# Decoder block on one core: the projection of q, k and v with the weights stationary, its row of factors by transposes, and the rotated rows moved by DMA

## The chip, the cores and the metric

The kernel runs on 1 core of one Trainium2 chip. The metric is the device time of an execution in microseconds (us), the median of the runs. TensorE (PE) multiplies, VectorE (DVE), ScalarE (ACT) and GpSimd (POOL) work on what lies beside it, and the queues of SP, ACT and POOL issue DMAs.

## What is computed

One layer on 1024 rows of width 1024: RMSNorm, one wide projection, a pooling mixer beside a sliding-window attention with sinks, merged by gates, and an MLP with squared ReLU. What the change touches is the projection to q, k and v, the partial rotation, and how they reach the attention:

```python
h = _rmsnorm(x, g_mix_pre[l])
proj = jnp.einsum('bsd,de->bse', h, w_in[l]) + b_in[l]
u_pool, q, k, v, gates = jnp.split(proj, IN_SPLITS, axis=-1)
q = _partial_rotary(q.reshape(B, S, N_Q_HEADS, HEAD_DIM), cos, sin)   # first 16 of 64 dims
k = _partial_rotary(k.reshape(B, S, N_KV_HEADS, HEAD_DIM), cos, sin)
v = v.reshape(B, S, N_KV_HEADS, HEAD_DIM)
y_attn = _sliding_window_sink_attention(q, k, v, attn_sinks[l])       # 8 q heads, 2 kv heads
```

## The kernel before

Every float32 operand is split into a high and a low part (`split`: a cast on ACT, a difference on DVE), and each product is made in three passes (`PASSES`). x comes transposed (`xt`, eight tiles k of 128 features by 1024 rows), is scaled by the norm's gain and split (`scaled`, L201 to L204). The norm's factor of each row, `r1`, is not known yet: the sums of squares come from a second read of x by rows (`square_row`, L211), and the factor is put in where the products leave PSUM.

**The projection.** `mm_q` (L178) and `mm_kv` (L188) take a tile n of 128 rows of x as the stationary operand and stream the weights: 512 columns for q, 256 for k and v. The loop over k (L216 on) does this for n = 0 to 3 as the tiles arrive. The products lie with the rows on the partitions. `pre_q` and `pre_kv` (L311, L314) multiply by the row's factor, a scalar of each partition, and add the bias; `rotate` turns the first 16 dims of each head, on DVE for n = 0 and on POOL for the others; `post_qkv` (L339) transposes q (four, L344) and k (one, L345) with PE, so that the features come to lie on the partitions, splits them, and prepares v on POOL. `make_rb` writes the eight factors of each partition to DRAM and reads them back as one row `rb` on all partitions, for the gates.

**The order.** Behind the loop the order on PE, DVE and ACT is that of the code (`manual_schedule`). The attention of tile n is `score_all(n)` (L388), `softmax_max`, `softmax_exp`, `softmax_scale` (L420), `attend_t` (transposes of the probabilities, L431), `attend_own`, `attend_v` (L456). Between these, `fill(t)` takes work for PE from the stream `others()`: the projection of n = 4 to 7, then halves of the gates' products (`half`, L583 through `gt.mm`), until about t us are spent. In step n of the loop stand `attend_t(n)`, the exponentials and the scale of n + 1, `attend_v(n)`, the scores of n + 2, and `post_qkv(n + 3)`.

Of the kernel before, what the change touches and what calls it, by code (L numbers as in the profile page):

```python
# [8 lines left out]
F32 = mybir.dt.float32  # L9
# [27 lines left out]
C_COS = C_MASK + 2 * P  # L37
C_SIN = C_COS + NT * 8
C_CNT = C_SIN + NT * 8
# [7 lines left out]
V_N = V_ONE + 1  # L47
# [3 lines left out]
def block_kernel(ctx: ExitStack, tc, xt, x, consts, vecs, sinks, b_qkv, g_post, g_mlp, g_mlp_post,  # L51
# [95 lines left out]
    cst = cp.tile([P, C_N], F32, name="cst")  # L147
# [32 lines left out]
    def mm_q(n, k, bq):  # L180
        for j, (xh, h) in enumerate(PASSES):
            pe.matmul(bq, xs_[k][n // 4][:, xh, n % 4 * P:(n % 4 + 1) * P], wq[k][:, h, :],  # L182
                      start=k == 0 and j == 0, stop=k == NK - 1 and j == 2)

    def bkv_of(n):
        return bkv[n // 2 * 2][:, n % 2, :] if n < 4 else bkv[n][:, 0, :]

    def mm_kv(n, k, joint=False):  # L188

        for j, (xh, h) in enumerate(PASSES):  # L190
            pe.matmul(bkv_of(n), xs_[k][n // 4][:, xh, n % 4 * P:(n % 4 + 1) * P],  # L191
                      wkv[k // 2][:, h, k % 2, :], start=k == 0 and j == 0 and not (joint and n % 2),
                      stop=k == NK - 1 and j == 2 and not (joint and n % 2 == 0))

    bq01, bq23 = bank("sc", [2, 512]), bank("sc", [2, 512])
    bq = {0: bq01[:, 0, :], 1: bq01[:, 1, :], 2: bq23[:, 0, :], 3: bq23[:, 1, :]}
    bz = bank("mm")
    bkv = {0: bank("mm", [2, 256]), 2: bank("mm", [2, 256])}
    for j in range(9):
        pe.matmul(bz, zeros[:, :P], zeros, start=j == 0, stop=j == 8)  # L200
    def scaled(t, xs, gk, th, a, b):  # L201
        src = xs[:, th * 512 + a:th * 512 + b]
        act.activation(t[:, 0, a:b], src, AF.Identity, scale=gk)
        dve.scalar_tensor_tensor(t[:, 1, a:b], src, gk, f32(t[:, 0, a:b]), ALU.mult, ALU.subtract)  # L204


    later = []

    ssq = small()

    def square_row(n):  # L211
        t = at(*(("qkv", 3) if n % 2 == 0 else ("s4", 4)), [S])
        nc.sync.dma_start(t, x[n])
        act.activation(t, t, AF.Square, accum_out=ssq[:, n:n + 1])

    for k in range(NK):  # L216
        xs = at("s4", 4, [S])
        ws = stage([768]) if k else ws_first
        if k < 2:
            if k == 0:  # L220
                nc.sync.dma_start(vec, vecs)
            for a, b in ((0, 256), (256, 512)) if k == 0 else ((0, 512),):
                nc.sync.dma_start(xs[:, a:b], xt[k][:, a:b])
            if k:
                nc.sync.dma_start(ws, w_qkv[k])
            else:
                nc.sync.dma_start(ws[:, 512:], w_qkv[k][:, 512:])
            later.append((k, xs))
        else:
            nc.sync.dma_start(xs, xt[k])  # L230
            nc.sync.dma_start(ws, w_qkv[k])
            if k == 2:
                for i, t in later:
                    nc.sync.dma_start(t[:, 512:], xt[i][:, 512:])
        halves_ = [xp.tile([P, 2, 512], F32R, tag="x", name=nm("x")) for _ in range(2)]
        gk = vec[:, V_G + k:V_G + k + 1]
        q = wslot([2, 512]) if k < 6 else ga_.tile([P, 2, 512], F32R, tag="ga", name=nm("wq"))
        if k % 2 == 0:
            wkv.append(ga_.tile([P, 2, 2, 256], F32R, tag="ga", name=nm("wkv")))
        kv = wkv[-1]  # L240
        first = k == 0
        if first:
            split(q[:, 0, :], q[:, 1, :], ws[:, :512], first=dve)
        for a, b in ((0, 256), (256, 512)) if first else ((0, 512),):
            scaled(halves_[0], xs, gk, 0, a, b)
        if not first:
            split(q[:, 0, :], q[:, 1, :], ws[:, :512])
        split(kv[:, 0, k % 2, :], kv[:, 1, k % 2, :], ws[:, 512:])
        if k >= 2:
            scaled(halves_[1], xs, gk, 1, 0, 512)  # L250
        xs_.append(halves_)
        wq.append(q)
        for n in range(4):
            mm_q(n, k, bq[n])
        for n in range(4):
            mm_kv(n, k, joint=True)
        if k == 2:
            for i, t in later:
                scaled(xs_[i][1], t, vec[:, V_G + i:V_G + i + 1], 1, 0, 512)
        if k >= 5:  # L260
            square_row(k - 5)
    for n in range(3, NT):
        square_row(n)
    nc.sync.dma_start(cst, consts)
    nc.sync.dma_start(snk, sinks.unsqueeze(0).broadcast_to([P, NH]))
    bq_b = bcast(b_qkv, 768)
    dve.tensor_scalar(nsnk, snk, -1.0, None, ALU.mult)
# [35 lines left out]
    tfs = {}  # L303

    def tf_of(n):
        if n not in tfs:
            tfs[n] = flat(yy.tile([P, 2, 512], F32, tag="y", name=nm("tf"))) if n in (2, 3, 7) else at("qkv", 3, [1024])
        return tfs[n]

    def pre_q(n):  # L310
        dve.scalar_tensor_tensor(tf_of(n)[:, :512], bq[n], r1[:, n:n + 1], bq_b[:, :512], ALU.mult, ALU.add)  # L311

    def pre_kv(n):
        dve.scalar_tensor_tensor(tf_of(n)[:, 512:768], bkv_of(n), r1[:, n:n + 1], bq_b[:, 512:768], ALU.mult, ALU.add)  # L314

    def rotate(n):
        tf = tf_of(n)
        t = tf[:, :768].rearrange("p (h d) -> p h d", d=HD)
        c = cst[:, C_COS + 8 * n:C_COS + 8 * n + 8].unsqueeze(1).unsqueeze(1).broadcast_to([P, 10, 2, 8])
        s = cst[:, C_SIN + 8 * n:C_SIN + 8 * n + 8].unsqueeze(1).unsqueeze(1).broadcast_to([P, 10, 2, 8])  # L320
        rot = t[:, :10, :ROT].rearrange("p h (a b) -> p h a b", a=2)
        a = tf[:, 768:928].rearrange("p (h a b) -> p h a b", a=2, b=8)
        b = sp.tile([P, 10, 2, 8], F32, tag="rb", name=nm("rb"), bufs=1)
        eng = pool if n else dve
        eng.tensor_tensor(a, rot, c, ALU.mult)
        eng.tensor_tensor(b, rot, s, ALU.mult)
        eng.tensor_tensor(rot[:, :, 0, :], a[:, :, 0, :], b[:, :, 1, :], ALU.subtract)
        eng.tensor_tensor(rot[:, :, 1, :], a[:, :, 1, :], b[:, :, 0, :], ALU.add)

    vfs = {}  # L330
# [8 lines left out]
    def post_qkv(n):  # L339
        tf = tfs.pop(n)  # L340
        t = tf[:, :768].rearrange("p (h d) -> p h d", d=HD)
        bt, bk = bank("mm"), bank("mm")
        for m in range(4):
            pe.transpose(bt[:, m * P:(m + 1) * P], tf[:, m * P:(m + 1) * P], ident)  # L344
        pe.transpose(bk[:, :P], tf[:, 512:640], ident)  # L345
        qt = at("qt", 2, [2, 512], F32R)
        split(qt[:, 0, :], qt[:, 1, :], bt)
        ks = slice(n * P, (n + 1) * P)
        split(khi[:, ks], klo[:, ks], bk[:, :P])
        qts[n] = qt  # L350

# [380 lines left out]
    def others():  # L732
        for n in range(4, NT):
            bq[n] = bank("mm")
            for k in range(NK):
# [4 lines left out]
                if k == NK - 1:  # L740
                    pre_q(n)
# [1692 lines left out]
```

## Time and profile before

| | us |
|---|---|
| runs of the kernel before (3) | 1086.58, 1087.01, 2804.63; median 1087.01 |
| the profiled execution's own time | 1086.91 |
| its span, first to last instruction | 1085.1 |
| mean granted TensorE clock | 0.998 of full speed |
| busy: PE, DVE, ACT, POOL | 1076.7, 891.9, 635.5, 102.9 |
| DMA, mean over the span | 223 GB/s |

The span is what the profiler saw of the program's instructions; the time also has what lies around it. A timeline row gives an instruction's start and length, and how many of a kind follow one another; as matmuls and many others overlap their successors, the distance from start to start prices a stream. Groups give busy time and the mean length of one. One of the three runs stands far from the other two; the median does not use it.

### The profile page before, as it was taken

The page shows a single profiled execution, that of the slowest core. Times are in us where ns is not written, and L with a number is a line of the kernel's source. Part 1 is how long each engine was busy: PE and PEld are TensorE (multiplying, and loading weights), DVE is VectorE, ACT ScalarE, POOL GpSimd, SP SyncE. Part 2 cuts the span into 40 slices and gives each one's busy share as a digit, 9 for nine tenths or more (in the row PEclk, how much of TensorE's full clock was granted, in tenths as well). Part 3 has the DMA queues.
Part 4 walks back from the last instruction along what each step waited for, and adds up shares of the span by engine and source line. Part 5 has one row for each costly group of instructions (what it writes and reads, how often), then busy time and mean ns, then how long its engine had stood idle before and what let it go on. Part 6 is the DMA issues. An engine that isn't in the chain of part 4 may idle for free.

```text
span 1085.1 us, 14912 instructions
## 1 busy us (share of the span) xinstructions
PE 1076.7 (99%) x5355; PEld 907.9 (84%) x5355; DVE 891.9 (82%) x1294; ACT 635.5 (59%) x1058; POOL 102.9 (9%) x174
## 2 busy tenths in 40 slices
PE   9999999999999999999999999999999999999997
PEld 8888888888888888888888888888888899899886
DVE  6688888989887887879979867776757899898997
ACT  7567886456654247587666555555544474275553
POOL 0354410100100012100000000001000000000000
PEclk9999999999999999999999999999999999999999
DMA  9656899679865776822576654655898687459842
GB/s 339 200 170 176 214 250 349 191 233 312 260 216 178 220 200 137 291 84 92 191 253 242 251 207 161 227 184 212 294 393 274 217 274 255 151 175 331 300 140 78
DMA packets 106618, 242.06 MB, mean 223 GB/s; under 512 B 11056, under 2 KB 28592, under 8 KB 106544
## 3 DMA queue, kind: packets, MB, share of 16 engines
q1 hardware_dynamic: 86528, 191.69, 51.6%
q0 software_dynamic: 14112, 29.37, 11.5%
q10 hardware_dynamic: 5904, 20.06, 4.7%
q8 instruction: 42, 0.69, 0.2%
q14 instruction: 32, 0.26, 0.1%
HBM read 166.63 MB, written 73.40 MB: 221 GB/s over the span
## 4 chain that ended last, share of the span: by engine, by line
PE 94%; DVE 2%; ACT 2%; DMA 1%; issue 1%; SPq 0%; DVEq 0%; ACTq 0%
PE mm L583 26%; PE at L583 19%; PE at L2129 12%; PE mm L2129 5%; PE mm L1523 5%; PE at L2103 4%; PE mm L2103 4%; PE mm L494 3%; PE sc L182 2%; PE at L1523 2%; PE at L1251 2%; PE mm L191 2%; PE mm L182 2%; PE mm L1251 2%; PE mm L496 1%; PE sc L456 1%
## 5 line engine op out<-in xcount | busy, mean ns | idle before, releaser
L2129 PE MATMUL at<-ar,wh 128*128 128x512 f32 x564 | 134.6, 389 | 0.0
L2129 PEld LDWEIGHTS at<-ar,wh 128*128 128x128 f32 x564 | 105.8, 188 | 22.2 <-DVE ar L104 0.3
L101 ACT CAST wh<-raw 128x1024 fp32r<-128x1024 f32 (+1 forms) x54 | 53.4, 988 | 79.9 <-PE at L2129 51.3
L104 DVE TENSOR_TENSOR wh<-st,wh 128x512 fp32r<-128x512 f32 (+1 forms) x106 | 76.4, 730 | 25.0 <-ACT wh L101 21.2
L583 PE MATMUL mm<-T,wx 128*128 128x512 f32 x375 | 90.9, 390 | 0.0
L104 DVE TENSOR_TENSOR wh<-raw,wh 128x1024 fp32r<-128x1024 f32 (+1 forms) x54 | 61.6, 1142 | 29.4 <-ACT wh L101 29.1
L583 PEld LDWEIGHTS mm<-T,wx 128*128 128x128 f32 x375 | 70.2, 188 | 15.1 <-DVE wx L104 0.6
L101 ACT CAST wh<-st 128x512 fp32r<-128x512 f32 (+2 forms) x105 | 67.6, 653 | 19.4 <-DVE st L539 5.8
L583 PE MATMUL mm<-gr,wh 128*128 128x512 f32 x321 | 77.4, 391 | 0.0
L583 PEld LDWEIGHTS mm<-gr,wh 128*128 128x128 f32 x321 | 59.9, 188 | 12.2
L2129 PE MATMUL mm<-ar,wh 128*128 128x512 f32 x276 | 69.6, 389 | 0.0
L583 PE MATMUL mm<-T,wh 128*128 128x512 f32 x267 | 66.1, 389 | 0.0
L101 ACT CAST ar<-B 128x1024 fp32r<-128x1024 f32 (+2 forms) x59 | 43.0, 757 | 30.7 <-PE mm L2129 14.8
L2129 PEld LDWEIGHTS mm<-ar,wh 128*128 128x128 f32 x276 | 51.8, 188 | 10.7
L583 PE MATMUL at<-gr,wh 128*128 128x512 f32 x243 | 59.0, 389 | 0.0
L583 PEld LDWEIGHTS mm<-T,wh 128*128 128x128 f32 x267 | 50.1, 188 | 10.5
L583 PE MATMUL mm<-x,wh 128*128 128x512 f32 x240 | 58.9, 394 | 0.0
L583 PEld LDWEIGHTS at<-gr,wh 128*128 128x128 f32 x243 | 45.6, 188 | 9.5
L583 PEld LDWEIGHTS mm<-x,wh 128*128 128x128 f32 x240 | 44.2, 188 | 9.6 <-ACT f L692 0.2
L583 PE MATMUL at<-T,wx 128*128 128x512 f32 x213 | 52.2, 389 | 0.0
L104 DVE TENSOR_TENSOR ar<-B,ar 128x1024 fp32r<-128x1024 f32 (+2 forms) x59 | 49.1, 855 | 1.1 <-ACT ar L101 1.1
L2103 PE MATMUL at<-ar,wh 128*128 128x256 f32 x336 | 47.5, 283 | 0.0
(556 smaller groups left out, 2461.2 us busy)
## 6 DMA issues: line engine op xcount, KB each, us to landing
raw<-f_dram SPq DMA_DIRECT2D x40, 512.0 KB, 4.2
B<-in_w_dn_dram SPq DMA_DIRECT2D x32, 512.0 KB, 6.6
st<-in_w_up_dram SPq DMA_DIRECT2D x27, 512.0 KB, 5.0
f_dram<-g SPq DMA_DIRECT2D x21, 512.0 KB, 2.9
wh<-f_dram SPq DMA_DIRECT2D x20, 512.0 KB, 5.8
g<-spill_dram SPq DMA_DIRECT2D x17, 512.0 KB, 6.0
st<-in_w_g_dram SPq DMA_DIRECT2D x16, 512.0 KB, 5.0
f_dram<-g ACTq DMA_DIRECT2D x16, 512.0 KB, 3.8
```

Of the source, the lines that this page charges most:

```text
L101: act.copy(hi, src)
L104: return eng.tensor_tensor(lo, src, f32(hi), ALU.subtract)
L182: pe.matmul(bq, xs_[k][n // 4][:, xh, n % 4 * P:(n % 4 + 1) * P], wq[k][:, h, :], start=k == 0 and j == 0, stop=k == NK - 1 and j == 2)
L191: pe.matmul(bkv_of(n), xs_[k][n // 4][:, xh, n % 4 * P:(n % 4 + 1) * P], wkv[k // 2][:, h, k % 2, :], start=k == 0 and j == 0 and not (joi ...
L456: pe.matmul(yb[:, kv], v[:, c:c + P], p[ph][:, 4 * kv:4 * kv + 4].rearrange("p i q -> p (i q)"), start=j < 2, stop=j >= len(mms) - 2)
L494: pe.matmul(bs[th], whi[:, k, :], rhs(k, hl, th), start=k == 0 and hl == 0, stop=False)
L496: pe.matmul(bs[th], wlo[:, k, :], rhs(k, 0, th), start=False, stop=k == nk - 1)
L583: pe.matmul(b, w[wh][:, kt, :], x_, start=not after and kt == 0 and j == 0, stop=kt == 3 and j == 2, skip_group_check=after)
L1251: pe.matmul(b, w[wh][:, kt, :], xo[xh][:, kt, :], start=not after and kt == 0 and j == 0, stop=kt == 1 and j == 2, skip_group_check=after)
L1523: pe.matmul(bs[t], Am[a][k][ah][:, t * P:(t + 1) * P], Wm[w][k][wh], start=not after and k == 0 and j == 0, stop=k == 3 and j == 2, skip_g ...
L2103: pe.matmul(part[q][:, t, :], o[fs][fh][:, fk, t * P:(t + 1) * P], o[ws][wh][:, wk, :], start=q not in onto and (s_, t, j) == (0, 0, 0), s ...
L2129: pe.matmul(bs[t], fo[fh][:, k2, t * P:(t + 1) * P], wo_[wh][:, k2, :], start=not after and s2 == 0 and k2 == 0 and j == 0, stop=(s2, k2) ...
```

## The change

The columns of the projection are put into six groups f of 128 features, and the weights are the stationary operand (`mm_in`): a product is 128 features by 512 rows, so q and k lie with features on the partitions from the start and are not transposed. Groups 0 to 3 hold the parts of two q heads that are not rotated, 48 and 48, with 32 features of v between them; groups 4 and 5 hold the first and second halves of the rotated dims of all heads (80 features each) and 48 of the rest of k. The first 512 rows (th = 0) are projected while the tiles arrive, the others (th = 1) in `others()`.

Because a row's factor now varies along the free dimension, the row `rb` is needed ahead of the first product that leaves PSUM. `factors(th)` makes the factors of half th and spreads them, and `make_rb(th)` turns them into a row on all partitions by four transposes. `close_in` multiplies by it (DVE) and adds the bias, one per partition (ACT). `turn` and `turn_end` rotate groups 4 and 5 as a whole, on DVE for th = 0 and on POOL for th = 1. The rotated rows then move by DMA (`rows_in`, `keys_rest`) into the places between the others that v's rows held, after v's have been moved (`values_out`) to a tile `tv`; for th = 0 v is read from a tile of its own (`unbiased`), which holds the products ahead of the bias. `split_q(n)` splits q of 128 rows, `split_k` k of 512, and `post_v` transposes v, once per tile. Tables of the rotation come from a new input; the tile of `cst` keeps its old size without them, and the tiles behind it their addresses.

```diff
+    def mm_in(f, th, k, a=0, b=512):
+        for j, (wh, xh) in enumerate(PASSES):
+            pe.matmul(b_in[f, th][:, a:b], w_in_of(f, k, wh), xs_[k][th][:, xh, a:b],
+                      start=k == 0 and j == 0 and a == 0, stop=k == NK - 1 and j == 2)
...
+    def factors(th):
+        n = slice(4 * th, 4 * th + 4)
+        rsqrt(r1[:, n], ssq[:, n], 4)
+        t = rows_of[th] = at("s4", 4, [2, 512])[:, 0, :]
+        dve.tensor_copy(t.rearrange("p (n k) -> p n k", k=P), r1[:, n].unsqueeze(2).broadcast_to([P, 4, P]))
+
+    def make_rb(th):
+        b, t = bank("mm"), rows_of.pop(th)
+        for n in range(4):
+            pe.transpose(b[:, n * P:(n + 1) * P], t[:, n * P:(n + 1) * P], ident)
+        act.copy(rb[:, th * 512:(th + 1) * 512], b)
...
+        for f in (4, 5, 0, 1):
+            for k in (6, 7):
+                mm_in(f, 0, k)
+        nc.sync.dma_start(cst, consts)
         for n in range(4):
+            square_row(n, at("qkv", 3, [S]) if n < 3 else at("s4", 4, [S]))
+        load_table(0)
+        factors(0)
...
+    def close_in(f, th):
+        raw_in(f, th)
+        t = o = raw_of(f, th)
+        if f < 4 and not th:
+            if f % 2 == 0:
+                unbiased[f // 2] = wide_s8()
+            t = unbiased[f // 2][:, f % 2]
+        dve.tensor_tensor(t, b_in.pop((f, th)), rb[:, th * 512:(th + 1) * 512], ALU.mult)
+        act.activation(o, t, AF.Identity, bias=vec[:, V_BQ + f:V_BQ + f + 1])
...
+    def turn(th, eng):
+        t, tab = raw_r[th][:NR], tables.pop(th)
+        turned[th] = [at("s4", 4, [2, 512])[:NR] for _ in range(2)]
+        for i, o in enumerate(turned[th]):
+            eng.tensor_tensor(o, t, tab[:NR, i, :].unsqueeze(1).broadcast_to([NR, 2, 512]), ALU.mult)
+
+    def turn_end(th, eng):
+        t, (a, b) = raw_r[th][:NR], turned.pop(th)
+        eng.tensor_tensor(t[:, 0], a[:, 0], b[:, 1], ALU.subtract)
+        eng.tensor_tensor(t[:, 1], a[:, 1], b[:, 0], ALU.add)
+
+    MOVES = ((0, 0, 16, 56), (1, 0, 8, 48), (1, 8, 16, 72))
+
+    def rows_in(q, th, dst, m):
+        for i, a, b, to in MOVES:
+            q.dma_start(dst[to:to + b - a], raw_r[th][16 * m + a:16 * m + b, i, :])
...
+    def split_q(n):
+        qt = qts[n] = at("qt", 2, [2, 512], F32R)
+        for i, src in enumerate(raw_q[n // 4]):
+            hi, lo = (qt[:, h, i * 256:(i + 1) * 256].rearrange("p (m k) -> p m k", k=P) for h in range(2))
+            split(hi, lo, src[:, :, n % 4 * P:(n % 4 + 1) * P])
...
     def others():
-        for n in range(4, NT):
-            bq[n] = bank("mm")
+        for f in (4, 5, 0, 1, 2, 3):
+            b_in[f, 1] = bank("mm")
             for k in range(NK):
-                mm_q(n, k, bq[n])
+                mm_in(f, 1, k)
...
+                    close_in(f, 1)
+                    if f == 5:
+                        keys_rest(nc.sync, 1)
+                        turn(1, pool)
+                        turn_end(1, pool)
+                        rows_in(nc.sync, 1, raw_k[1], 4)
+                    elif f < 4:
+                        values_out(nc.sync, 1, f)
+                    if f in (1, 2, 3):
+                        rows_in(nc.sync, 1, raw_of(f - 1, 1), f - 1)
+                    if f == 1:
+                        split_k(1)
...
-        rsqrt(r1, ssq[:, :NT], NT)
-        make_rb()
+        make_rb(0)
+        for f in (2, 3):
+            for k in (6, 7):
+                mm_in(f, 0, k)
+        for n in range(4, NT):
+            act.activation(squares_late[n], squares_late[n], AF.Square, accum_out=ssq[:, n:n + 1])
+        close_in(4, 0)
+        close_in(5, 0)
+        turn(0, dve)
+        keys_rest(nc.sync, 0)
+        turn_end(0, dve)
+        rows_in(nc.sync, 0, raw_k[0], 4)
+        for m in range(4):
+            close_in(m, 0)
+            rows_in((nc.sync, nc.scalar, nc.scalar, nc.gpsimd)[m], 0, raw_of(m, 0), m)
+        for m in range(4):
+            values_out(nc.gpsimd, 0, m)
+        load_table(1)
+        factors(1)
+        fill(4.0)
+        make_rb(1)
         act.activation(warm, r1[:, :1], AF.Exp)
...
+        split_k(0)
+        fill(6.5)
+        split_q(0)
+        fill(1.6)
         score_all(0)
...
                 hurry[0] = False
+                if n + 2 < NT:
+                    split_q(n + 2)
...
-            if n + 3 < NT:
-                post_qkv(n + 3)
+            if n + 2 < NT:
+                post_v(n + 2)
```

TensorE between the end of the first half's projection and the first transposes behind it, before. `mm_502` and `mm_529` are tile 4 of q and of k and v; `mm_551` and `mm_552` are the transposes of tile 0:

```order
L191 MATMUL mm_102<-wkv_365,x_405 128x256 x6
L182 MATMUL mm_502<-wh_120,x_119 128x512 x3
L182 MATMUL mm_502<-wh_160,x_159 128x512 x3
...
L182 MATMUL mm_502<-wq_364,x_363 128x512 x3
L182 MATMUL mm_502<-wq_407,x_406 128x512 x3
L191 MATMUL mm_529<-wkv_121,x_119 128x256 x3
L344 MATMUL mm_551<-cst,qkv_488 128x128 x4
L345 MATMUL mm_552<-cst,qkv_488 128x128
```

The same place now, from the first factor row (`mm_444`) to the second (`mm_545`); `sc_99` are groups 2 and 3 of th = 0, `mm_526` is group 4 of th = 1:

```order
L224 MATMUL mm_444<-cst,s_56_394 128x128 x4
L187 MATMUL sc_99<-x_323,wq_325 128x512 x3
L187 MATMUL sc_99<-x_335,wq_337 128x512 x3
L187 MATMUL sc_99<-x_323,wq_325 128x512 x3
L187 MATMUL sc_99<-x_335,wq_337 128x512 x3
L187 MATMUL mm_526<-x_124,wkv_118 128x512 x3
L187 MATMUL mm_526<-x_168,wkv_118 128x512 x3
L187 MATMUL mm_526<-x_200,wkv_195 128x512 x3
L187 MATMUL mm_526<-x_230,wkv_195 128x512 x3
L187 MATMUL mm_526<-x_262,wkv_257 128x512 x3
L187 MATMUL mm_526<-x_292,wkv_257 128x512 x3
L224 MATMUL mm_545<-cst,s_83_524 128x128 x4
```

The transposes of q and k are gone, and two groups of transposes of factors have come, with twelve and eighteen matmuls between them.

ScalarE at the same place, before: from the last square of a row of x to the first cast of split queries:

```order
L214 ACTIVATE s_59_455,sm_112<-s_59_455 128x1024
L109 ACT_TABLE_LOAD
L109 ACTIVATE sm_474<-sm_112,eps 128x8
L897 ACT_TABLE_LOAD
L897 ACTIVATE warm_93<-r_86 128x1
L101 CAST qt_558<-mm_551 128x512
```

Now, from the copy of the first factor row to that of the second (`mm_444`, `mm_545`); L949 are squares, L351 biases, L372 the moves of rotated rows that ACT issues, L109 the root for the second factors:

```order
L225 COPY rb_all<-mm_444 128x512
L949 ACTIVATE s_61_424,ssq<-s_61_424 128x1024
...
L949 ACTIVATE s_64_430,ssq<-s_64_430 128x1024
L351 ACTIVATE qkv_466<-qkv_466,vec 128x512 x2
L351 ACTIVATE qkv_483<-s_75_484,vec 128x512 x2
L372 DMA qkv_483<-qkv_466 16x512
L372 DMA qkv_483<-qkv_466 8x512 x2
L351 ACTIVATE qkv_495<-s_77_496,vec 128x512
L372 DMA qkv_495<-qkv_466 16x512
...
L351 ACTIVATE qkv_495<-s_77_496,vec 128x512
L109 ACTIVATE sm_513<-ssq,eps 128x4
L225 COPY rb_all<-mm_545 128x512
```

Before, one root stood behind all squares; now the second one stands behind four squares, six biases and six issues of moves.

VectorE from the scale of step n + 1 = 3 to the mask of the scores of tile 4, before:

```order
L420 TENSOR_TENSOR s_159_1084<-s_159_1084,den_1153 128x1024
L104 TENSOR_TENSOR wh_1202<-st_1075,wh_1202 128x512
L104 TENSOR_TENSOR wh_1239<-st_1075,wh_1239 128x512
L397 COPY_PREDICATED s_190_1248<-cst,sc_1249 128x2x256
L397 COPY_PREDICATED s_190_1248<-cst,sc_1263 128x2x256
L708 SCALAR_TENSOR_TENSOR wh_1237<-st_1077,vec,wh_1236 128x1024
```

and now:

```order
L471 TENSOR_TENSOR s_156_1062<-s_156_1062,den_1117 128x1024
L104 TENSOR_TENSOR wh_1155<-st_997,wh_1155 128x512
L104 TENSOR_TENSOR wh_1172<-st_1095,wh_1172 128x512
L751 SCALAR_TENSOR_TENSOR wh_1184<-st_999,vec,wh_1183 128x1024
L104 TENSOR_TENSOR qt_1193<-q_684,qt_1193 128x256
L104 TENSOR_TENSOR qt_1193<-s_121_853,qt_1193 128x256
L448 COPY_PREDICATED s_189_1226<-cst,sc_1227 128x2x256
```

The split of tile 4's queries (`qt_1193`) has come ahead of the mask of the very scores that read it, and a third product of weights with it; before, it was made a step earlier.

284 lines of the change are left out of this document (130 added, 154 removed).

## The prediction

> **What bounds the kernel now.** The page was read first: engine totals, then the chain that ended last.
>
> ```profile
> PE 1076.7 (99%) x5355; PEld 907.9 (84%) x5355; DVE 891.9 (82%) x1294; ACT 635.5 (59%) x1058; POOL 102.9 (9%) x174
> ...
> PE 94%; DVE 2%; ACT 2%; DMA 1%; issue 1%; SPq 0%; DVEq 0%; ACTq 0%
> ```
>
> TensorE has almost no idle time, and the chain is nearly all TensorE. Busy time by stage (PE, PEld, DVE, ACT, POOL, clock, DMA share, GB/s) says where the change works:
>
> ```profile
> 0.00:40.00 40.00, 39.13 (x207) 33.56 (x208) 21.56 (x45) 30.99 (x54) 1.36 (x12) 1.00 0.90 333
> 40.00:160.00 120.00, 119.63 (x751) 100.47 (x750) 104.66 (x158) 82.49 (x231) 50.59 (x94) 1.00 0.71 189
> ```
>
> The first 40 us hold the projection of rows 0 to 511, the next 120 the rest of it and the attention. TensorE waits 0.37 us in those 120, while VectorE is busy for 104.66: TensorE is the bound, VectorE close behind. So the change is worth what it takes from TensorE's stream, less every wait that it puts in there. Behind this part the changed program has the same instructions in the same order.
>
> **TensorE's stream.** Its timeline (start, length) prices the instructions:
>
> ```profile
> 0.78 4.18 PE L200 MATMUL mm<-const-float32-0.0 128*128 128x512 f32 x9 [0.78 <-PEq L2420]
> ...
> 34.64 2.91 PE L182 MATMUL sc<-wq,x 128*128 128x512 f32 x12
> 37.39 1.60 PE L191 MATMUL mm<-wkv,x 128*128 128x256 f32 x12
> 38.82 4.27 PE L182 MATMUL mm<-wh,x 128*128 128x512 f32 x18
> 42.93 1.52 PE L182 MATMUL mm<-wq,x 128*128 128x512 f32 x6
> 44.29 0.52 PE L191 MATMUL mm<-wkv,x 128*128 128x256 f32 x3
> 44.64 0.60 PE L344 MATMUL mm<-cst,qkv 128*128 128x128 f32 x4
> 45.08 0.27 PE L345 MATMUL mm<-cst,qkv 128*128 128x128 f32 x1
> 45.11 2.76 PE L191 MATMUL mm<-wkv,x 128*128 128x256 f32 x21
> ```
>
> Lengths overlap, so starts are used. Eighteen 512-wide matmuls take 42.93 - 38.82 = 4.11, 0.228 each; twelve 256-wide ones 38.82 - 37.39 = 1.43, 0.119 each; five transposes 45.11 - 44.64 = 0.47, four of them 0.44, 0.11 each. Removed: 192 matmuls of 256 columns, 192 x 0.119 = 22.9. Added: 96 of 512, 21.9. At k = 0 twelve wide ones become 24 narrow: +0.1. The 192 matmuls of q stay 192, with operands exchanged. Forty transposes in eight groups (3.8) become 8 for v and 8 for the two factor rows (16 x 0.11 = 1.8): -2.0. Sum: **-2.9 us**, all on the path. Bounds: -2.0 (only the transposes gain) and -3.0.
>
> **A wait at the second factor row.** Now each half has its own factors, turned into a row by four transposes (make_rb). The second ones stand on TensorE behind only 12 + 18 matmuls after the first: with the first four transposes 0.44 + 30 x 0.228 = 7.3 us of work. What feeds them is ScalarE's square root for rows 512 to 1023, which stands in ScalarE's row behind everything that follows the first factor row. Prices, ScalarE:
>
> ```profile
> 0.74 0.40 ACTq L156 DMA_DIRECT2D st<-in_w_qkv_dram  x1
> ...
> 23.19 1.34 ACT L203 ACTIVATE x<-s,vec 128x512 fp32r<-128x512 f32 x2 [1.39 <-DMA s<-in_xt_dram]
> ...
> 34.14 1.06 ACT L214 ACTIVATE qkv<-qkv 128x1024 f32<-128x1024 f32 x1
> 35.10 0.18 ACT L214 ACTIVATION_READ_ACCUMULATOR qkv<-qkv 128x1 f32 x1
> ...
> 37.91 0.30 ACT L109 ACTIVATE sm<-sm,eps 128x8 f32<-128x8 f32 x1
> ```
>
> and its groups by shape (busy, mean ns):
>
> ```profile
> L692 ACT COPY f<-mm 128x512 f32<-128x512 f32 x16 | 9.2, 578 | 0.7 <-PE mm L583 0.7
> ...
> L101 ACT CAST wkv<-st 128x256 fp32r<-128x256 f32 x8 | 3.2, 402 | 0.4 <-DMA st<-in_w_qkv_dram 0.4
> ```
>
> VectorE, timeline and groups:
>
> ```profile
> 3.65 0.43 DVE L103 CAST wh<-st 128x512 fp32r<-128x512 f32 x1 [2.73 <-DMA st<-in_w_qkv_dram]
> ...
> 38.24 0.20 DVE L113 RECIPROCAL sm<-sm 128x8 f32<-128x8 f32 x1 [1.23 <-ACT sm L109]
> ...
> 39.34 0.88 DVE L314 SCALAR_TENSOR_TENSOR qkv<-mm,r,bc 128x256 f32<-128x256 f32 x2
> ...
> 47.13 0.68 DVE L104 TENSOR_TENSOR qt<-mm,qt 128x512 fp32r<-128x512 f32 x1
> ```
>
> ```profile
> L420 DVE TENSOR_TENSOR s<-s,den 128x1024 f32<-128x1024 f32 x8 | 10.2, 1274 | 0.3
> ...
> L104 DVE TENSOR_TENSOR wkv<-st,wkv 128x256 fp32r<-128x256 f32 x8 | 3.4, 419 | 0.3 <-ACT wkv L101 0.3
> ```
>
> The chain, from the first four transposes: their result 0.60; ScalarE's copy 0.58; four squares of rows 512 to 1023, 4 x 1.24 = 5.0; bias of groups 4 and 5, 2 x 0.67 = 1.3 (VectorE's products run beside the squares); VectorE's two rotations, 2 x 1.27 = 2.5, and two differences, 1.4; products of groups 0 and 1, 1.4; bias of 1, 0.7; three DMA issues, 1.2; bias of 2, 0.7; three issues, 1.2; bias of 3, 0.7; root 0.30; the rest of the inverse root 39.34 - 38.24 = 1.1; spreading it 0.43. Sum 19.1, less about 0.5 for back-to-back lengths that overlap: 18.6. TensorE has 7.3: it waits **+11.3 us**. Bounds: if the six issues cost nothing, 8.9; if one of them also waits for an earlier small move to land (2.5, row below), 13.8. Behind the waiting transposes TensorE's whole queue stands, nobody else has work for it.
>
> **The restart.** The only row in which TensorE starts from rest is the first: nine 512-wide matmuls in 4.18 us, where 9 x 0.228 = 2.1 would do. I take this **+2.0** for the restart after 11 us; bounds 0 (no row shows a restart later on) and 2.1. The granted clock reads 1.00 in the window of that row too, so that column does not tell. The Trainium skill speaks against the change here: "TensorE: Matmul & The Clock Gate", Part 1, says that the array's clock is halved after an idle window of some 3.4 us and comes back after about as long under load. The trace agrees at its start; no run here shows a later restart. By that rule the sum comes out as below, 1102.2; without it, at 1100.2.
>
> **The attention steps.** Before, the split queries of step n+2 were made a whole step ahead, from transposed tiles. Now split_q(n+2) is issued just ahead of the scores that read it, behind softmax_scale(n+1) on VectorE. Where these stand before (scale on VectorE, then the scores' first matmul):
>
> ```profile
> 81.99 1.22 DVE L420 TENSOR_TENSOR s<-s,den 128x1024 f32<-128x1024 f32 x1
> ...
> 96.49 1.52 DVE L420 TENSOR_TENSOR s<-s,den 128x1024 f32<-128x1024 f32 x1
> ...
> 109.88 1.22 DVE L420 TENSOR_TENSOR s<-s,den 128x1024 f32<-128x1024 f32 x1
> ```
>
> ```profile
> 85.49 0.39 PE L388 MATMUL sc<-klo,qt 64*128 64x256 f32 x2
> ...
> 98.19 0.39 PE L388 MATMUL sc<-klo,qt 64*128 64x256 f32 x2
> ...
> 111.07 0.39 PE L388 MATMUL sc<-klo,qt 64*128 64x256 f32 x2
> ```
>
> Slack from the scale's end to the scores: 2.3, 0.2 and 0.0 us at steps n = 1, 2, 3. In it must now fit: at n = 1 a product and a bias (0.68 + 0.67), a cast 0.40, two differences 0.84 and three weight splits that now stand ahead (3 x 0.68), 4.6; at n = 2 three such and the two differences, 2.9; at n = 3 one and two, 1.5. Late by 2.3, 2.7 and 1.5: 6.5 if each makes TensorE wait, 2.7 if the first waits give the later ones room. VectorE's free time is 13% of a 12.7 us step, 1.6; the sum less one such recovery is 4.9, so **+4.9**, between the ends 0 and 6.5.
>
> **At nothing.** The scores of step 0: behind the second factor row TensorE has 42 matmuls, 9.6 us; its last operand needs 30 of them (6.8) and then product, bias, cast and two differences, 2.6, so 9.4. If that cover fails it costs the excess. Half 2's rotation goes to GpSimd:
>
> ```profile
> 47.51 0.35 POOL L327 TENSOR_TENSOR qkv<-qkv,rb 128x80 f32<-128x80 f32 x1
> 47.82 0.36 POOL L328 TENSOR_TENSOR qkv<-qkv,rb 128x80 f32<-128x80 f32 x1
> 48.13 0.54 POOL L325 TENSOR_TENSOR tf<-tf,cst 128x160 f32<-128x160 f32 x1
> 48.61 0.98 POOL L326 TENSOR_TENSOR rb<-tf,cst 128x160 f32<-128x160 f32 x1
> ```
>
> ```profile
> spill_dram<-st SPq DMA_DIRECT2D x8, 256.0 KB, 2.5
> ```
>
> Carried on by column (0.35 to 0.54 over 80), two of 1024 and two of 512 take 2 x 2.6 + 2 x 1.4 = 8.0; at the slow row's 0.98 for 0.54, 14.5. Its rows then move (three issues 1.2, landing 2.5). They are due when ScalarE reaches the second half's keys, two groups of 24 matmuls and two sets of scores later: 10.9 + some 3 = 14, estimated. 11.7 fits. The added moves of half 1 on SP and GpSimd start during the chain above and land inside the 9.6 us of cover. On SP they stand ahead of four stores of summed weights, half 2's ahead of loads of gate weights; at 0.4 an issue these come 3 to 5 us later, and are read a step or more after they land. The early phase needs less data before its matmuls than now (half of x), so no wait is added there.
>
> **The sum.** Against this execution's own time, 1086.9 (span 1085.1; the median of the runs is 1087.0, the same): 1086.9 - 2.9 + 11.3 + 2.0 + 4.9 = **1102.2 us**, 1.4% slower.
>
> **Rivals.** (1) The attention steps absorb the lateness: VectorE's 13% speaks for it, slack of 0.2 and 0.0 against. 1102.2 - 4.9 = 1097.3. (2) GpSimd rotates at its slow rate: 14.5 + 3.7 = 18.2 against 14 of cover, and ScalarE's keys hold up the probabilities behind them: +4.2, 1106.4. For it: the slow rows occur while VectorE is busy. Against: it needs nearly all four instructions slow. (3) Faster: the second factor row comes in time and only the stream counts, 1086.9 - 2.9 = 1084.0. It decides when the chain is under 7.3 + 2.9 = 10.2 us instead of 18.6 and nothing else waits; the squares, the rotation and the DMA issues would all have to be out of its way. Against: ScalarE's row puts them ahead. That the change doesn't do what it says is out: the instruction counts on TensorE are 108 lower.
>
> **How the numbers follow.** Main case 0.42, (1) 0.28, (2) 0.13, (3) 0.13, other 0.04. Lower end: shortest wait, no restart cost, no step cost, 1086.9 - 2.9 + 8.9 = 1092.9, moved to 1090 for a part of the chain that overlaps. Upper: 1086.9 - 2.0 + 13.8 + 2.1 + 6.5 + 4.2 = 1111.5, rounded to 1111. Left out: (3) and the rest, under 0.2. About 2% (1108.7 upwards, 1065.3 downwards) is what a measurement of this kernel can tell from no change. Slower by more needs (2) with the long bounds: 0.09. Faster by more has no source: 0.01. Within: 0.90.
>
> **What would show it.** Right: TensorE idle some 11 us ahead of the second group of factor transposes, released by VectorE, with ScalarE in its DMA issues and biases meanwhile; matmuls of double pitch after it; TensorE waits of 1 to 3 us ahead of the scores of steps 3 to 5; no L191-like narrow matmuls. Wrong: no idle time at that place, or the root's instruction long done; GpSimd's rotation as releaser of ScalarE's keys would make it (2).

## The result, and the profile after

| | us |
|---|---|
| before, same chip (4 runs) | median 1087.59 |
| changed kernel (4 runs) | median 1124.28 (1123.72 to 1125.50) |
| ratio | 1.0342, 95% interval 1.0322 to 1.0362: slower |
| predicted | 1102.2 (1090 to 1111) |
| the profiled execution's own time, and its span | 1125.5, 1123.7 |

The sign and the first cause were as forecast; the loss is more than twice as large, and outside the range. The page of the changed kernel, totals and chain:

```profile
PE 1086.7 (97%) x5247; PEld 908.9 (81%) x5247; DVE 904.2 (80%) x1300; ACT 647.4 (58%) x1084; POOL 100.0 (9%) x149
...
PE 84%; DVE 6%; ACT 4%; DMA 3%; issue 2%; ACTq 0%; SPq 0%; DVEq 0%
```

TensorE runs 108 instructions fewer and is yet busy 10.0 us longer, and idle 28.6 us longer (1123.7 - 1086.7 = 37.0 against 8.4). By stage (PE, PEld, DVE, ACT, POOL, clock, DMA share, GB/s):

```profile
40.00:160.00 120.00, 93.12 (x473) 73.66 (x472) 78.88 (x115) 65.58 (x182) 32.73 (x48) 0.84 0.52 143
160.00:200.00 40.00, 38.25 (x211) 30.58 (x209) 36.65 (x48) 33.45 (x84) 15.02 (x23) 1.00 0.80 210
200.00:340.00 140.00, 139.66 (x617) 115.38 (x616) 126.16 (x160) 84.45 (x105) 15.31 (x17) 1.00 0.86 267
```

Nearly all of it lies between 40 and 200 us: 26.9 us of idle TensorE in the first row alone, where the kernel before had 0.4 (its TensorE is busy for all of the other two, 40.00 and 140.00); and there the granted clock is 0.84 instead of 1.00. VectorE does 78.88 us of work in that stretch instead of 104.66: it waits too. TensorE's waits, in total, times, longest:

```profile
PE mm L224 <- DVE s L218: 13.8, 1, 13.8
PE sc L439 <- DVE qt L104: 4.4, 4, 1.6
PE mm L626 <- ACT wh L101: 3.9, 1, 3.9
PE mm L763 <- ACT wh L748: 2.8, 1, 2.8
PE sc L439 <- ACT qt L101: 2.5, 2, 2.3
PE sc L507 <- DVE s L491: 0.8, 2, 0.5
...
PE sc L507 <- DVE s L104: 0.5, 1, 0.5
```

They are the second factor row, the split queries (two of 1.29 and 1.60 at the first scores, 2.29 at block 2, 1.7 us later on), the gate weights (3.94), the pooled branch's weights (2.78) and the masked probabilities. The clock is the other part. The trace records it as half of full speed (0.50 in the column behind GpSimd's) in five stretches. First the 3.41 us ahead of each of them, then the five:

```profile
42.37:45.78 3.41, 0.67 (x3) 0.21 (x2) 2.36 (x3) 0.98 (x2) 0.00 (x0) 1.00 0.54 168
69.68:73.09 3.41, 1.33 (x15) 0.93 (x14) 3.41 (x2) 0.58 (x1) 3.41 (x2) 1.00 0.67 183
96.99:100.40 3.41, 1.12 (x7) 0.62 (x5) 2.26 (x5) 1.19 (x3) 0.00 (x0) 1.00 0.49 159
110.64:114.05 3.41, 0.00 (x0) 0.00 (x0) 2.52 (x5) 0.79 (x2) 0.46 (x1) 1.00 0.50 113
127.71:131.12 3.41, 1.34 (x6) 0.76 (x5) 3.34 (x7) 3.41 (x11) 0.00 (x0) 1.00 1.06 384
```

```profile
45.78:62.85 17.07, 6.00 (x16) 4.88 (x17) 7.21 (x17) 6.27 (x10) 3.66 (x7) 0.50 0.23 55
73.09:79.92 6.83, 6.01 (x21) 4.93 (x22) 6.09 (x8) 1.80 (x4) 3.51 (x3) 0.50 0.05 10
100.40:103.81 3.41, 3.41 (x25) 2.94 (x26) 2.40 (x5) 2.46 (x5) 0.00 (x0) 0.50 0.37 74
114.05:117.46 3.41, 2.91 (x7) 2.29 (x8) 2.59 (x5) 2.58 (x6) 0.00 (x0) 0.50 0.31 84
131.12:137.94 6.82, 6.01 (x13) 4.32 (x14) 2.48 (x4) 1.80 (x4) 3.18 (x8) 0.50 1.01 315
```

The reader sees in the second column of the first block that TensorE was busy for 1.34 us or less of each 3.41 us, and then ran at half pace for 3.41 us or a multiple of it. In these stretches it is busy 24.3 us, half of which, 12.2, is lost. So the loss between the two profiled spans (38.6) is 28.6 us of idle time, plus 12.2 of half pace, less 2.2 that the stream gained (1086.7 - 12.2 = 1074.5 against 1076.7). The 2.2 is what is left over, not a measurement: the same working gives -2.3 in e5 and +0.9 in e12 below, which run the same matmuls. The granted clock over the span is 0.982 in this execution and 0.983 to 0.985 in the other three, which so had somewhat less half pace.

### The profile page after: what moved, and what is told of

It reads as the page before. It is cut to its first block, busy times and chain, and to the rows that moved or that the text cites. A ratio compares the mean times of both kernels' runs of the same rounds, so it can differ in the third digit from the quotient of the medians.

```text
span 1123.7 us, 14805 instructions
## 1 busy us (share of the span) xinstructions
PE 1086.7 (97%) x5247; PEld 908.9 (81%) x5247; DVE 904.2 (80%) x1300; ACT 647.4 (58%) x1084; POOL 100.0 (9%) x149
## 4 chain that ended last, share of the span: by engine, by line
PE 84%; DVE 6%; ACT 4%; DMA 3%; issue 2%; ACTq 0%; SPq 0%; DVEq 0%
PE mm L626 24%; PE at L626 18%; PE at L2193 12%; PE mm L2193 5%; PE mm L1587 5%; PE at L2167 4%; PE mm L2167 4%; PE mm L537 3%; PE at L1587 2%; PE at L1315 2%; PE mm L187 1%; PE mm L1315 1%; PE mm L539 1%; ACT s L465 1%; PE sc L439 1%
## 5 line engine op out<-in xcount | busy, mean ns | idle before, releaser
L626 PEld LDWEIGHTS mm<-gr,wh 128*128 128x128 f32 x321 | 59.9, 188 | 12.2
```

What stands on the lines that cost most here:

```text
L626: pe.matmul(b, w[wh][:, kt, :], x_, start=not after and kt == 0 and j == 0, stop=kt == 3 and j == 2, skip_group_check=after)
```

## The experiments

All times are medians of four runs; the ratio is to the kernel before on the same chip. The changed kernel has 1.0342 (1.0322 to 1.0362).

| run | median | ratio (95%) |
|---|---|---|
| e1 zeros in the wait | 1122.35 | 1.0327 (1.0310 to 1.0344) |
| e2 six DMA issues off ScalarE | 1119.27 | 1.0301 (1.0286 to 1.0316) |
| e3 rotation to be held, a new tile | 1142.02 | 1.0514 (1.0499 to 1.0530) |
| e4 query split earlier | 1125.64 | 1.0358 (1.0343 to 1.0374) |
| e5 root earlier | 1122.87 | 1.0334 (1.0316 to 1.0351) |
| e6 rotation held | 1123.90 | 1.0341 (1.0321 to 1.0361) |
| e7 an unused column | 1141.97 | 1.0511 (1.0495 to 1.0527) |
| e8 root earlier, 13 us of cover | 1117.86 | 1.0288 (1.0273 to 1.0303) |
| e9 scaling later | 1121.04 | 1.0317 (1.0302 to 1.0332) |
| e10 e2, e5, e6, e9, 10 us of cover | 1114.91 | 1.0253 (1.0236 to 1.0271) |
| e11 16 us, rotation on VectorE | 1131.27 | 1.0408 (1.0392 to 1.0423) |
| e12 24 us, rotation on VectorE | 1121.63 | 1.0322 (1.0304 to 1.0339) |
| e13 pooled weights earlier | 1126.42 | 1.0358 (1.0342 to 1.0373) |
| e14 the column, kernel before | 1105.42 | 1.0170 (1.0155 to 1.0185) |
| e15 all of e10, e13 and more | 1110.78 | 1.0209 (1.0189 to 1.0230) |

**e1: the idle time filled with zeros**

```diff
+        if th:
+            for j in range(56):
+                pe.matmul(b, zeros[:, :P], zeros, start=j == 0, stop=j == 55)
         for n in range(4):
             pe.transpose(b[:, n * P:(n + 1) * P], t[:, n * P:(n + 1) * P], ident)
```

> 56 matmuls of zeros (512 columns, 56 x 0.228 = 12.8 us) are put on TensorE into the bank of the second factor row, ahead of its transposes; they change no result. Theory A (the idle array's clock is halved, and what runs at half pace behind the wait is a cost of its own): the row still arrives at about 56.9 us, but the 42 matmuls behind it run at 0.228 instead of 0.313 for the first thirty; 2.5 to 2.9 us faster, 1121.6. Rival B (those matmuls are slow because their operands arrive late): no change of pace, 1124.3. Rival C: the pace is regained but TensorE then waits longer for the first scores' queries, 1124.3 with a longer wait there.

TensorE's timeline of e1:

```profile
42.87 12.40 PE L225 MATMUL mm<-const-float32-0.0 128*128 128x512 f32 x56
57.86 0.66 PE L227 MATMUL mm<-cst,s 128*128 128x128 f32 x4 [2.58 <-DVE s L218]
58.27 8.68 PE L187 MATMUL mm<-x,wkv 128*128 128x512 f32 x30
66.79 2.88 PE L187 MATMUL mm<-x,wh 128*128 128x512 f32 x12
```

The four transposes now take 0.66 us, at full pace (1.09 in the changed kernel), but 2.58 us of idle time were left, and the clock is at half for 3.41 us instead of 17.07, from 58.67 on: the thirty matmuls take 8.52 us, start to start, instead of 9.39 (6.84 at full pace). And the first scores wait as before for operands that come at 71.2 and 73.7. The intervals overlap, so the time decides nothing. The waits at the first scores (1.30 and 1.60) are not longer than before, which C asked for; what the pace gained, 0.87 us, went because the row came 1.0 us later in this execution (57.86, not 56.85). The pace hangs on the idle time, as A says.

**e2: what stands ahead of the root**

```diff
-            rows_in((nc.sync, nc.scalar, nc.scalar, nc.gpsimd)[m], 0, raw_of(m, 0), m)
+            rows_in((nc.sync, nc.gpsimd, nc.gpsimd, nc.gpsimd)[m], 0, raw_of(m, 0), m)
```

> The six row moves of groups 1 and 2 of the first half are issued by GpSimd instead of ScalarE; the same bytes move. Theory A (the root for rows 512 to 1023 is late because of what stands ahead of it in ScalarE's row, 4.4 us of it DMA issues): the idle time at the second factor row falls from 13.8 to some 9.4, and the time by 4 to 5 us, 1119.9. Rival B (the first scores are bound by the arrival of the same rows): the wait at the factor row falls, the wait at the first scores grows by as much, 1124.3.

ScalarE of the changed kernel, up to the root (L109):

```profile
47.70 1.33 ACT L351 ACTIVATE qkv<-s,vec 128x512 f32<-128x512 f32 x2 [4.35 <-DVE s L350]
49.07 2.52 ACTq L372 DMA_DIRECT2D qkv<-qkv  x3
51.63 0.72 ACT L351 ACTIVATE qkv<-s,vec 128x512 f32<-128x512 f32 x1 [2.59 <-DMA qkv<-qkv]
52.38 1.90 ACTq L372 DMA_DIRECT2D qkv<-qkv  x3
54.33 0.72 ACT L351 ACTIVATE qkv<-s,vec 128x512 f32<-128x512 f32 x1 [1.98 <-DMA qkv<-qkv]
54.96 0.28 ACT L109 ACTIVATE sm<-ssq,eps 128x4 f32<-128x4 f32 x1
```

and of e2:

```profile
47.32 2.56 ACT L351 ACTIVATE qkv<-s,vec 128x512 f32<-128x512 f32 x4 [4.35 <-DVE s L350]
49.79 0.28 ACT L109 ACTIVATE sm<-ssq,eps 128x4 f32<-128x4 f32 x1
```

Six issues cost 4.4 us, not the 2.4 that the prediction had; why one takes 0.74 us on the average here and 0.40 in the row that gave the price was not taken apart. Without them the wait is 8.8 instead of 13.8 us, and the time falls by 5.0: A. All the later waits stayed.

**e5: the root ahead of the rest**

```diff
         close_in(5, 0)
+        factors(1)
         turn(0, dve)
...
         load_table(1)
-        factors(1)
         fill(4.0)
```

> The square root for rows 512 to 1023 and the rest of their inverse root are issued right behind the biases of groups 4 and 5, ahead of the rotation, the products and biases of groups 0 to 3 and ScalarE's six DMA issues. Theory A (the wait at the second factor row is the root's place in ScalarE's row): the idle time there falls from 13.8 to 2 or 3 us. What follows is then bound by the first scores' operands (rows moved, query split), which come little earlier: a wait of 7 to 10 us ahead of the first scores takes its place, and the time falls by some 7, to 1117 (1113 to 1120). Rival B (additive): all 11 us are gained, 1113. Rival C (the first scores are bound by the rows' moves alone): 1124.

TensorE's timeline of e5, at the factor row and at the first scores:

```profile
44.89 0.63 PE L224 MATMUL mm<-cst,s 128*128 128x128 f32 x4 [2.14 <-DVE s L218]
...
65.86 0.48 PE L439 MATMUL sc<-klo,qt 64*128 64x128 f32 x2 [9.18 <-ACT qt L101]
```

and the product ahead of the query split on VectorE:

```profile
60.01 0.69 DVE L350 TENSOR_TENSOR qkv<-mm,rb_all 128x512 f32<-128x512 f32 x1 [9.29 <-DMA qkv<-qkv]
```

The root's place is the wait's cause (13.8 to 2.1 us), but the first scores start only 4 us earlier (69.8): VectorE stands 9.29 us until the rotated rows of the first half have been moved out of the place that the next product is written to, and TensorE waits 9.18 us at the first scores instead. Gained: 1.4 us, with overlapping intervals. A's mechanism held, but not its time: C's 1124, the first scores bound by the rows' moves, is nearer than A's 1117.

**e8: cover for that chain**

```diff
-        fill(6.5)
+        fill(13.0)
         split_q(0)
```

> As e5, and 13.0 instead of 6.5 us of the projection of rows 512 to 1023 stand ahead of the first query split, so that TensorE has work while the first scores' operands come. Theory A (what is missing at the first scores is cover): against e5 the wait at the first scores falls by up to 6.5 us, 1112. Rival B: the later waits for gate weights (3.9 and 2.8 us) grow by what is saved, since the stream reaches them 6.5 us earlier; 1117 as e5.

The first scores wait 4.6 instead of 9.2 us and 5.0 us are gained on e5. This is A's mechanism, short of its 1112: the gate weights are still waited for, 3.5 us, and now at 93 us, and waits of 1.95 and 2.49 us have come at the probabilities' products at 186 and 190 us. A part of what is saved comes back, as B says.

**e3, e7 and e14: the addresses**

```diff
         split_q(0)
+        pool.tensor_copy(small(1, "after"), f32(qts[0][:, 1, 511:512]))
+        turn(1, pool)
```

> GpSimd's rotation of the second half's keys is held until the second of the first query block's differences on VectorE is done (a copy of one column that reads it goes ahead). Theory A (VectorE's two differences take 4.89 us instead of 0.76 because GpSimd's two-input products run beside them): the two differences take 0.8 us, the waits of 1.29 and 1.60 at the first scores go, and with them the half pace that follows: 4 to 6 us faster, 1119. Rival B (VectorE is slow there for another reason, such as DMA traffic into the same memory): no change, 1124.3. Rival C: the second half's keys come too late and a wait appears at the later scores, 1124.3 or above.

e3 took 1142 and shows nothing of the rotation, because GpSimd's products started at 68.47 as before. Two controls, with only the tile and one memset of it (e7 in the changed kernel, whose edit is shown, and e14 in the kernel before):

```diff
+        pool.memset(small(1, "after"), 0.0)
```

> One unused column per buffer (three buffers of one number a partition) is added to a pool, and one memset of it on GpSimd; nothing else. It tests why e3 took 1142: theory A, the addresses of the tiles behind this pool move and the matmuls that read them take longer (395 instead of 389 ns in e3's largest group), 1141; rival B, e3's slowness came from its moved issues, then 1124.

> The kernel before with the unused column of e7 in the same pool and one memset of it; nothing else. Theory A (the matmuls' pace hangs on the addresses of the tiles behind that pool, in whichever kernel): slower by some 15 to 18 us, 1104, with 395 instead of 389 ns in the largest matmul group. Rival B (e7 met something that only the changed kernel has): 1087.

The largest matmul group of the kernel before:

```profile
L2129 PE MATMUL at<-ar,wh 128*128 128x512 f32 x564 | 134.6, 389 | 0.0
```

and of e14:

```profile
L2130 PE MATMUL at<-ar,wh 128*128 128x512 f32 x564 | 138.2, 395 | 0.0
```

An unused column costs some 18 us in either kernel, with matmuls of another phase 6 ns longer each. That it acts through the addresses is concluded from the edit, which touches nothing that those matmuls do; no trace shows an address. So e3 is set aside, and in all other runs the tiles keep their sizes and pools. The change itself kept them too: its group has 389 ns.

**e6: VectorE beside GpSimd**

```diff
+        if (f, th) == (5, 1):
+            late.append(lambda: act.activation(o, t, AF.Identity, bias=vec[:, V_BQ + f:V_BQ + f + 1]))
...
         score_all(0)
+        then.pop()()
```

> The bias of group 5 of the second half on ScalarE, and so GpSimd's rotation that needs it, is issued behind the copies of the first scores instead of ahead of the query split (in e3 GpSimd's two long products started at 68.47 as before, so that run held nothing). Theory A (VectorE's differences wait for GpSimd's products): the two differences take 0.8 instead of 4.9 us, the waits of 1.29 and 1.60 at the first scores go, so does the half pace of 6.8 us behind them; 4 to 6 us faster, 1119. Rival B (something else slows VectorE): the 4.9 us stay, 1124. Rival C: the second half's keys come late and a wait at later scores takes it back.

The changed kernel, GpSimd's long products and VectorE's differences of block 0:

```profile
68.72 4.85 POOL L360 TENSOR_TENSOR s<-qkv,s 80x1024 f32<-80x1024 f32 x2 [11.87 <-ACT qkv L351]
68.96 4.89 DVE L104 TENSOR_TENSOR qt<-qkv,qt 128x256 fp32r<-128x256 f32 x2 [1.09 <-ACT qt L101]
```

VectorE in e6, where the two products run from 70.93 to 75.67:

```profile
66.03 0.76 DVE L104 TENSOR_TENSOR qt<-qkv,qt 128x256 fp32r<-128x256 f32 x2
...
71.04 1.22 DVE L459 TENSOR_REDUCE nmx<-s 128x8 f32<-128x1024 f32 x1
72.29 1.05 DVE L460 SCALAR_TENSOR_TENSOR nmx<-nmx,nsnk 128x8 f32<-128x8 f32 x1
73.38 2.31 DVE L461 TENSOR_TENSOR es<-snk,nmx 128x8 f32<-128x8 f32 x1
75.61 1.83 DVE L104 TENSOR_TENSOR qt<-qkv,qt 128x256 fp32r<-128x256 f32 x2
```

A for the mechanism: alone, the differences take 0.76 us; and now operations on 8 columns take 1.05 and 2.31 us (0.17 each elsewhere), while the reduction with one input keeps its 1.22. In these rows a VectorE operation with two SBUF inputs ends about when GpSimd's product does (a product takes 2.4): it waits for it instead of sharing. The waits at the first scores are gone, and the half pace behind them; 1.4 us are given back at block 1's scores and 1.76 at the first probabilities, held up by those operations. The profiled execution ends 3.4 us earlier, but its four runs lie in two pairs, the profiled one in the first (1121.5 and 1122.1, 1125.8 and 1126.0), and the median gains nothing that can be told. The pairs differ in the granted clock too, 0.987 against 0.984 and 0.985: the second pair spent more time at half pace.

**e4 and e9: the steps of the attention**

```diff
+            if n + 2 < NT:
+                split_q(n + 2)
             if n + 1 < NT:
                 early = 1.0 if n > 2 else 0.0
```

> The split of the query block n+2 is issued right after the probabilities of step n are masked, ahead of the exponentials and the scaling of step n+1, instead of just ahead of its scores; same work. Theory A (the attention steps lose time because this split stands behind the scaling on VectorE): the wait of 2.29 us at the scores of block 2 goes, the half pace behind it too (1.7), and the later waits of 0.2 to 0.8; 4 to 6 us faster, 1119. Rival B (the next wait, 3.94 us for the gate weights, grows by what is saved): 1124.3, with a wait of over 6 us for the weights.

TensorE's timeline of e4:

```profile
98.75 0.39 PE L439 MATMUL sc<-klo,qt 64*128 64x256 f32 x2 [2.58 <-ACT yt L509]
...
112.42 2.93 PE L626 MATMUL mm<-x,wh 128*128 128x512 f32 x6 [4.56 <-ACT wh L101]
```

The wait for the queries became one of about the same length for a ScalarE copy, and the next ones grew (the gate weights to 4.56, not to the 6 that B named): B. ScalarE, not the split, was stuck, behind a bias whose product VectorE makes behind the scaling. So e9 moved the scaling:

```diff
-                softmax_scale(n + 1)
+                if n > 1:
+                    softmax_scale(n + 1)
...
                 fill((5.0 if n == 1 else 4.4) - early)
+                if n < 2:
+                    softmax_scale(n + 1)
```

> At the steps n = 0 and 1 alone, the scaling of step n+1's probabilities on VectorE is issued behind the projection work of its step instead of ahead of it, so that the products that close groups 2 and 3 of the second half stand ahead of the scaling; same work. Theory A (those products stand behind the scaling, their biases hold up ScalarE's row, and the query split and the casts of the gate weights stand behind the biases): the waits of 2.29 and 3.94 us shrink by 1 to 1.5 us each, and where they fall under some 1.9 us the half pace behind them goes too; 2 to 6 us faster, 1120. Rival B (the raw weights and the rows arrive late, the order on VectorE does not matter): 1124.

TensorE's timeline of e9, at the scores of block 2 and at the gate weights:

```profile
97.22 0.51 PE L439 MATMUL sc<-khi,qt 64*128 64x256 f32 x4 [0.53 <-DVE qt L104]
...
108.88 2.93 PE L626 MATMUL mm<-x,wh 128*128 128x512 f32 x6 [2.27 <-ACT wh L101]
```

2.29 became 0.53, 3.94 became 2.27, and the half pace at block 2 is gone: 3.2 us by the medians, as A says, though the intervals overlap a little. The two profiled executions lie 4.9 us apart, but 1.75 of it stands ahead of the edit, which acts only behind block 1's scores: these start at 80.77 instead of 82.52, because the half pace before them lasted 13.65 and 3.41 us instead of 17.07 and 6.83.

**e13: weights ahead of the exponentials**

```diff
                 early = 1.0 if n > 2 else 0.0
+                if n == 2:
+                    flush(lazy)
```

> At step n = 2 the split of the pooled branch's weights (a ScalarE pass and a VectorE pass) is issued ahead of the exponentials instead of where its first use forces it, behind eight exponentials and two more casts; same work. Theory A (the changed kernel runs its projection some 4.4 us further ahead of the attention than the kernel before, by the sum of its covers, and so reaches weights ahead of the place where the hand-made order prepares them): the wait of 2.78 us goes, the half pace of 6.8 us behind it too; 4 to 6 us faster, 1119. Rival B (ScalarE has no room there, the exponentials and what follows are late by what is saved): 1123 to 1124.

The wait of 2.78 became one of 0.64, but ScalarE then reached the next group's pass ahead of its load:

```profile
141.53 1.15 ACT L748 ACTIVATE wh<-st,vec 128x1024 fp32r<-128x1024 f32 x1 [5.56 <-DMA st<-in_w_bp_dram]
```

TensorE paid 2.57 us at 147.6 and 6.8 us of half pace there instead. B, by a wait that neither theory had; the intervals overlap.

**e10, e11, e12 and e15: several together**

> e2, e5, e6 and e9 together, with 10.0 us of cover ahead of the first query split (6.5 in the change, 13.0 in e8). Theory A (the causes are separate and each of them gives what it is worth once the next one behind it is gone too): the second factor row waits 2 us, the first scores 0 to 3 us, no half pace at either; 1105 to 1110. Rival B (the first scores are bound by one chain, rows moved and landed, that none of the four shortens but e2): 1114. Neither reaches the kernel before, 1087, since the waits for gate weights stay.

> e2, e5 and e9 together; the second half's rotation on VectorE instead of GpSimd (3.9 us more on VectorE, and GpSimd's two-input products, beside which a VectorE operation on 8 columns took 2.31 instead of 0.17 us in e6, are gone); 16 us of cover ahead of the first query split. Theory A (the loss is a chain of late operands and lacks cover): against e10 (1114.9) the waits at the first scores (2.8 and 0.5) and the 3.5 ahead of the first probabilities' transposes go, with the half pace behind them; 1104 to 1109. Rival B (what is saved comes back as waits for gate weights and for the later blocks' rows): 1113 to 1117.

> As e11, with 24 us of cover. Theory A: the same or better than e11, 1100 to 1107, since nearly the whole projection of the second half then stands ahead of the attention. Rival B: VectorE and ScalarE idle in the longer cover and their work of the attention (VectorE is busy for 105 of 120 us at that stage in the kernel before) starts 8 us later, so waits return in the later steps: 1110 to 1115.

> e2, e5, e6, e9 and e13 together, 10.0 us of cover ahead of the first query split, GpSimd's rotation held until behind the second block's query split, the second half's keys split when group 2 closes instead of group 1. Theory A (each cause costs its own wait, and half pace behind each wait of over 1.9 us): the waits of 2.8, 3.5 and 1.7 us that e10 had at the first blocks shrink; 1105 (1102 to 1110). Rival B (VectorE, busy for 87% at this stage before, has become the bound, and every piece moved ahead of another delays that one): 1114 as e10.

e10 brings the first scores from 69.8 to 60.7 us, as A says, though with 3.4 us of half pace behind them, which A did not expect; it gains 9.4 us, which is B's time: its longest wait, 3.5 us, now stands at the first probabilities. e11 and e12 missed both of theirs. In e12 TensorE waits only 1.3 us between its first matmuls and 78 us, and then at nearly every step up to 195: the cover was taken from the work that stood there, and the attention starts no earlier (72.2). e11 is the slowest of the four, and slower than the change itself, with a wait of 4.8 us for gate weights and one of 3.95 at later scores; why 16 us are worse than 24 was not taken apart. e15 gains 13.5 us, the most, just short of A's range, and is still 2.1% (1.9 to 2.3) slower than the kernel before: TensorE has four stretches of 3.4 us and one of 6.8 at half pace, and its longest wait is 2.9. No run beats the kernel before.

## Why the prediction was wrong

- **The stream, -2.9.** -2.2 by what is left over, within its bounds; but between -2.3 and +0.9 in the runs with the same matmuls, so the size is not settled.
- **The second factor row, +11.3.** Mechanism and place held: 13.8 us, the upper bound, 2.0 of the missing 2.5 because the issues took 4.4 us, not 2.4 (e2). The bound assumed one wait for a landing instead, so that it was met is luck. That its end is all gain, which rival (3) needed, is refuted by e5: with 2.1 us left there, the moved rows hold the first scores.
- **The restart, +2.0.** This is the step that failed most. For one restart it was about right (9.39 - 6.84 = 2.6 us, and the transposes), but I charged it once, as a matter of the long idle time, and put no price on it behind waits of 2 us. It occurs five times: 12.2 us, 10.2 more than the term.
- **The attention steps, +4.9.** 4.0 us were measured for split queries behind block 0. That this is near 4.9 is luck: the largest, 2.29, stands at block 2, which the sum left out (it starts at n = 1, whose scores are block 3's), while blocks 3 and 4 wait for nothing and block 5 for 1.0. The cause is VectorE's order, as I argued, and more by the closing product than by the split (e4, e9).
- **At nothing: the first scores.** 2.9 us, with 6.8 us at half pace behind. My cover of 9.6 against 9.4 took the differences at their price alone; beside GpSimd's products they took 4.89 instead of 0.76 (e6). GpSimd itself needed 7.9 us, as I had carried on (8.0), so rival (2) looked at the right instruction for the wrong victim.
- **At nothing: loads and casts of the weights behind.** 6.7 us of waits and 10.2 us at half pace. I followed their loads, not the ScalarE passes that split them. The gate weights' casts stand behind the same late biases (e9: 3.94 became 2.27); the pooled branch's pass stood behind the exponentials (e13), and e9 left its 2.78 as it was. The masked probabilities add 1.3 us of waits that no term had. The sum of the covers ahead of the loop grew from 18.2 to 22.6 us, so TensorE reaches these weights some 4.4 us further ahead of the attention than the hand-made order was set for; that this shift alone would do it was not tried by itself.
- **The chances.** 0.09 for slower by over 2% asked for one more mechanism with long bounds. Several small waits that each start a half pace were not among the cases.

On the clock, the sum by the Trainium skill's "TensorE: Matmul & The Clock Gate", Part 1, was nearer than the one without it. The trace agrees on the halving and on steps of some 3.4 us (3.41 here), but not on an idle window being needed: a busy time of 1.34 of 3.41 us was not enough to keep the clock.

What stays open: 23.8 us in e15. In its trace TensorE is idle for 24.4 us (8.4 before) and busy for 20.2 us at half pace, 10.1 of which are lost; what would take the rest of these waits away was not found. VectorE's share of it as a bound (it has 89.7 us of work between 40 and 160 us there, against 104.66 before) was not separated from the order of the queues.

## What to carry to other kernels

Price a wait on TensorE as the wait and what runs at half pace behind it: waits of 2.3 to 2.8 us here cost 4 to 6. Where a chain gains a link (a bias on another engine, a move by DMA), list what stands behind that link in every queue that it passes, not only who reads its result. Where two profiles are compared, see first how far they lie apart ahead of the edit (1.75 us in e9). And before comparing two variants, see that tiles which neither touches keep their addresses, or run a control that only moves them.

## What was not expected of the hardware

- One unused number per buffer in a pool moved the tiles behind it, and 512-wide matmuls of later phases took 395 instead of 389 ns: some +18 us in both kernels (e7, e14). That the tiles moved is concluded, not seen, and which address makes the difference was not tried.
- A VectorE operation on 8 columns took 2.31 us beside a GpSimd product, 0.17 otherwise (e6); with one input it was not slowed. The Trainium skill's "GPSIMD Engine Reference", Specifications, says that GpSimd's SBUF interfaces are shared with VectorE, with contention from VectorE instructions that have two SBUF inputs. The trace agrees, and here the operation waited about until GpSimd's had ended.
- Half pace began after windows of 3.41 us with 1.34 us of matmuls or less in the changed kernel, also where the longest single wait in the window was 1.3 us (the first scores). Half pace lasted 3.41 us or a multiple of it, and how much of it fell on the same wait differed between executions (6.83 us at the first scores in the changed kernel, 3.41 in e9).
